# A last unit whose second block of positions is finished in two halves of 256 columns

## The chip, the cores and the metric

The kernel runs on one core of one Trainium2 chip. Its time is the device time in microseconds of one execution, and the median over several executions is quoted. The engines that matter here are TensorE (PE in the profile: matmuls; PEld is its weight load), VectorE (DVE), ScalarE (ACT), GpSimd (POOL) and SyncE (SP), whose queue issues every DMA of this kernel. Each engine takes its instructions in the order in which they stand in its own queue; between engines they wait on semaphores.

## The reference

One layer of a hybrid decoder block: a mixer (gated linear attention beside a short convolution) with a residual add, a SwiGLU feed-forward net with a residual add, and a last RMSNorm. 2048 positions, width 1024, feed-forward width 2816, float32. What the change touches is the end:

```python
        h2 = rmsnorm(x, norm2_g[l])
        ffn = (jax.nn.silu(h2 @ w_ffn_gate[l]) * (h2 @ w_ffn_up[l])) @ w_ffn_down[l]
        x = x + ffn
    return rmsnorm(x, norm_f_g)
```

with `rmsnorm(x, g) = x * rsqrt(mean(x * x) + 1e-6) * g`, the mean over the 1024 features of a position.

## The kernel before

**Layout.** Everything is held with features on the 128 partitions and positions along the free axis. `KD = 8` tiles of 128 features (index `d`) times `NB = 4` blocks of `PB = 512` positions make the whole residual stream. The feed-forward net is done for one half of the positions at a time (two blocks, `j = 0, 1`), so `y[d, j]` is a tile of 128 features by 512 positions; the tiles of one `d` lie side by side in one buffer (for `d = 7` in two).

**Products.** A float32 factor is split into a high and a low part, and a product of two 128-wide blocks is three matmuls (`product_step`, L366 to L368: high by high, high by low, low by high), each with a weight load of its own. Most matrix products go through `unit` (L370), a seven-product scheme in place of eight for a 2 by 2 block problem, with a few additions on GpSimd and VectorE. The down projection `ffn_down` (L921) takes the feed-forward width in four groups, and within a group four units, one for each pair of features `d0, d0 + 1`; what a unit gives is added to `y` (L965). In the last group of the last half the squares of each finished `y[d, j]` are summed into `ssq[j]` (L772 on ScalarE for the first, then L775 on ScalarE and L776 on GpSimd).

**The last unit.** `last_unit` (L995) is the last of these sixteen units. It does not use the seven-product scheme but eight plain products, so that the block `j = 0` is complete before `j = 1` is begun: four accumulations in PSUM (`j` outer, `r` inner, `d = 6 + r`), each of 2 by 3 calls of `product_step`, that is 18 matmuls of 512 columns. After each, VectorE adds the result to `y` (L1036), ScalarE squares it (L1038) and multiplies `y` by the norm's weight (`gain`, L1005; the gains of the tiles `d < 6` are done earlier, beside the unit ahead). The squares of `d = 6` are added to `ssq[j]` by GpSimd (L1041); those of `d = 7` come in by a second matmul. `norm` (L1007) adds over the partitions with a float32 matmul by a tile of ones into `tot` (L1010, L1011), takes the logarithm and the exponential on ScalarE (L184, L185), refines the result in one Newton step on VectorE (L186, L163, L164, L165) and leaves the factor in a PSUM tile `rb`, of which ScalarE makes a copy in SBUF (L1013) since GpSimd multiplies from SBUF. `scale` (L1016) multiplies the eight tiles of the block by the factor, two on GpSimd and six on VectorE, and each is stored as soon as it is done (L148).

**What sets the order.** The kernel is written as straight code for one core, and the tile layer's scheduler places the instructions of each engine by a timeline that it estimates while it builds the program; it may take an instruction ahead of others on its engine. `tc.issue_after(x)` holds the next instructions behind `x`. In the last unit before, only the accumulations of TensorE are chained in this way. ScalarE's table for logarithm and exponential is loaded (L1002) after the last weight split. The stores all go through SP's queue in one order, and ahead of each stands a wait for the store eight places earlier, whose semaphore it uses again.

Of the kernel before, what the change touches and what calls it, by code (L numbers as in the profile page):

```python
# [13 lines left out]
AF = mybir.ActivationFunctionType  # L14
ALU = mybir.AluOpType
# [3 lines left out]
P = 128  # L19
D = 1024  # L20
SEQ = 2048
PB = 512
NB = SEQ // PB
KD = D // P
# [7 lines left out]
EPS = 1e-6  # L32
# [14 lines left out]
C_G1, C_G2, C_GF, C_BG, C_GN, C_CW = 0, 8, 16, 24, 26, 27  # L47
# [4 lines left out]
def tile_hymba_block(ctx, tc, x, xt, win, wa, wgu, wout, wffn, wdown, wdown_first, small, out):  # L52
    nc = tc.nc
    act, dve, pool, pe = nc.scalar, nc.vector, nc.gpsimd, nc.tensor

    def pool_of(name, bufs, **kw):
# [19 lines left out]
    ones = const.tile([P, P], F32, name="ones")  # L76
# [4 lines left out]
        out=mask[:], in_=mask[:], compare_op=ALU.is_ge, fill=0.0, base=0,  # L81
# [65 lines left out]
    def store(dst, src):  # L147
        return nc.sync.dma_start(dst, src)  # L148
# [33 lines left out]
    def finish_rstd(v, tot, n, rb=None):  # L182
        l, y0 = bt("l"), bt("y0")
        act.activation(l[:], tot[:], AF.Ln, bias=eps[:], scale=1.0 / n)  # L184
# [173 lines left out]
        w["A22"] = weight_quarter(a22)  # L358
        return w

    def product_step(o, w, op, k, first):
        n = len(op)
        c = slice(k * P, (k + 1) * P)
        wh, wl = w[:, 0, c], w[:, 1, c]
        xh, xl = op[k][:, 0, :], op[k][:, 1, :]
        pe.matmul(o[:], wh, xh, start=first and k == 0, stop=False, skip_group_check=True)  # L366
        pe.matmul(o[:], wh, xl, start=False, stop=False, skip_group_check=True)  # L367
        return pe.matmul(o[:], wl, xh, start=False, stop=k == n - 1, skip_group_check=True)  # L368

    def unit(src, ops, into=None):  # L370

# [89 lines left out]
    rbs, raws, first_weights, last_load, rows, squares = {}, {}, {}, [], {}, {}  # L461
# [211 lines left out]
    done = set()  # L673
# [321 lines left out]
    def last_unit(src, ops, b12, y, ssq):  # L995


        raw = raw_weights(src)
        w = [weight_quarter(raw[:, i, :]) for i in (0, 1, 3, 2)]
        columns = (ops["B11"], ops["B21"]), (b12, ops["B22"])  # L1000
        with tc.issue_after(last_hi[0].ins):
            act.preload_act_table_set("natural_log_exp_and_others")  # L1002

        def gain(d, j):
            act.activation(y[d, j], y[d, j], AF.Copy, scale=col(C_GF + d))  # L1005

        def norm(j, q):  # L1007

            tot, rb = bank("tot"), bank("rb")
            pe.matmul(tot[:], ones[:], ssq[j][:], start=True, stop=False)  # L1010
            pe.matmul(tot[:], ones[:], q[:], start=False, stop=True)  # L1011
            finish_rstd(ssq[j], tot, D, rb)
            act.activation(ssq[j][:], rb[:], AF.Copy)  # L1013
            return rb

        def scale(j, rb):  # L1016
            for d in range(KD):
                eng, by = (pool, ssq[j]) if d in (2, 5) else (dve, rb)
                eng.tensor_tensor(y[d, j], y[d, j], by[:], ALU.mult)
                store(out[2 + j, :, d, :], y[d, j])  # L1020

        for d in range(KD - 2):
            for j in range(2):
                gain(d, j)
        q, rbs = {}, []
        for j in range(2):
            for r in range(2):
                o = bank()
                with ExitStack() as stack:
                    if j or r:  # L1030
                        stack.enter_context(tc.issue_after(done.ins))
                    for i in range(2):
                        for k in range(len(b12)):
                            done = product_step(o, w[2 * r + i], columns[j][i], k, i == 0)
                yy = y[KD - 2 + r, j]
                dve.tensor_tensor(yy, o[:], yy, ALU.add)  # L1036
                q[j] = tt("q")
                act.activation(q[j][:], yy, AF.Square)  # L1038
                gain(KD - 2 + r, j)
                if not r:  # L1040
                    pool.tensor_tensor(ssq[j][:], ssq[j][:], q[j][:], ALU.add)  # L1041
                if j and not r:
                    rbs.append(norm(0, q[0]))
        rbs.append(norm(1, q[1]))
        for j in range(2):
            scale(j, rbs[j])


    act.preload_act_table_set("natural_log_exp_and_others")
# [3 lines left out]
    ops, first, differences = build_h()  # L1053
# [132 lines left out]
```

## Time and profile before

| what | us |
|---|---|
| median of 3 executions | 2110.91 (2108.93 to 2113.38) |
| span of the profiled execution (first to last instruction) | 2109.1 |
| TensorE busy in it | 2033.1 (96%) |
| VectorE, ScalarE, GpSimd busy | 1418.4, 1014.1, 972.4 |
| last matmul of the last product starts | 2089.04 |
| first instruction of the last block's scalings | 2100.72 |
| last store is issued | 2105.30 |

Of the profiled execution the profile gives only the span; the median of the executions is 1.8 us above it. All times in the text below are microseconds from the start of that span. In the timeline a row has the start, the duration, the engine, the line and operation, what it writes and reads, how many instructions it stands for, and in brackets how long the engine was idle before it and what ended the wait. A matmul's duration includes its way through the array, so that one matmul begins before the one ahead has ended: the distance of the starts is what it costs.

### The profile page before, as it was taken

How to read it: one execution, taken by the hardware profiler on the slowest of the kernel's cores; microseconds unless marked ns; L12 is line 12 of the kernel's file. 1: busy time of each engine (PE TensorE's matmuls, PEld its weight loads, DVE VectorE, ACT ScalarE, POOL GpSimd, SP SyncE). 2: the span in 40 equal slices, each digit the busy share in tenths (PEclk: the TensorE clock that was granted, in tenths of full speed). 3: DMA queues.
4: the chain of work that ended last, by engine and by line, in shares of the span. 5: the costliest groups of instructions: out<-in, count | busy, mean ns of one | idle time of the engine just before them, and what ended most of it. 6: DMA issues, size and time to landing. Idle time of an engine off the chain costs nothing.

```text
span 2109.1 us, 26874 instructions
## 1 busy us (share of the span) xinstructions
PE 2033.1 (96%) x9133; PEld 1648.9 (78%) x9133; DVE 1418.4 (67%) x1983; ACT 1014.1 (48%) x1997; POOL 972.4 (46%) x703
## 2 busy tenths in 40 slices
PE   5999999999999999999999999999999989999996
PEld 4778888877888878788888878787888868877775
DVE  7669786549753786788786665554766666665564
ACT  5555455656542356445545443333554554543344
POOL 3436322222102464564464348764645544436774
PEclk9999999999999999999999999999999999999998
DMA  7349485425586872656545687697454535587763
GB/s 277 126 158 318 139 329 164 148 83 164 201 284 235 325 249 100 241 198 221 217 172 220 243 327 272 235 338 296 158 207 179 206 134 190 183 344 281 269 269 110
DMA packets 189241, 464.43 MB, mean 220 GB/s; under 512 B 19824, under 2 KB 65072, under 8 KB 179504
## 3 DMA queue, kind: packets, MB, share of 16 engines
q1 hardware_dynamic: 189104, 462.72, 60.4%
q8 instruction: 72, 1.18, 0.2%
q14 instruction: 65, 0.53, 0.1%
HBM read 297.49 MB, written 165.15 MB: 219 GB/s over the span
## 4 chain that ended last, share of the span: by engine, by line
PE 70%; DVE 8%; DMA 7%; ACT 3%; issue 3%; POOL 2%; SPq 0%; DVEq 0%; ACTq 0%; POOLq 0%
PE mm L366 21%; PE mm L368 21%; PE mm L367 21%; DVE wq L154 2%; DMA op<-shT 1%; DVE so L154 1%; PE mm L794 1%; DVE h L490 1%; PE mm L795 1%; PE mm L797 1%; DVE op L154 1%; DMA sx<-y 1%; ACT wq L153 1%; PE o_ps L718 1%; DMA shT<-so 1%
## 5 line engine op out<-in xcount | busy, mean ns | idle before, releaser
L366 PE MATMUL mm<-op,wq 128*128 128x512 f32 x2499 | 981.3, 395 | 23.8 <-DVE c L390 7.8
L368 PE MATMUL mm<-op,wq 128*128 128x512 f32 x2499 | 966.1, 392 | 12.6 <-DVE wq L154 11.9
L367 PE MATMUL mm<-op,wq 128*128 128x512 f32 x2499 | 976.0, 391 | 0.0
L154 DVE TENSOR_TENSOR wq<-raw,wq 128x512 fp32r<-128x512 f32 (+2 forms) x626 | 527.3, 849 | 329.9 <-ACT wq L153 324.3
L153 ACT ACTIVATE wq<-raw 128x512 fp32r<-128x512 f32 (+2 forms) x626 | 363.6, 587 | 555.8 <-PE mm L368 402.4
L366 PEld LDWEIGHTS mm<-op,wq 128*128 128x128 f32 x2499 | 470.8, 188 | 137.6 <-ACT wq L153 12.3
L368 PEld LDWEIGHTS mm<-op,wq 128*128 128x128 f32 x2499 | 470.5, 188 | 123.5 <-DVE wq L154 24.8
L367 PEld LDWEIGHTS mm<-op,wq 128*128 128x128 f32 x2499 | 471.2, 189 | 96.7 <-issue 1.0
L351 POOL TENSOR_TENSOR raw<-s,raw 128x512 f32<-128x512 f32 (+2 forms) x97 | 127.5, 1314 | 422.2 <-DVE wq L154 402.0
L390 DVE TENSOR_TENSOR c<-mm,c 128x512 f32<-128x512 f32 x267 | 183.0, 686 | 95.7 <-PE mm L368 93.0
L349 POOL TENSOR_TENSOR s<-raw 128x512 f32<-128x512 f32 (+2 forms) x97 | 130.2, 1343 | 216.2 <-DMA raw<-in_wffn_dram 88.8
L356 POOL TENSOR_TENSOR raw<-raw 128x512 f32<-128x512 f32 (+2 forms) x97 | 126.7, 1306 | 135.3 <-DVE wq L154 128.1
L386 ACT ACTIVATE c<-mm 128x512 f32<-128x512 f32 x267 | 154.7, 585 | 38.0 <-PE mm L368 36.8
L776 POOL TENSOR_TENSOR ssx<-ssx,q 128x512 f32<-128x512 f32 x52 | 76.5, 1483 | 156.0 <-ACT q L775 155.8
L350 POOL TENSOR_TENSOR raw<-raw 128x512 f32<-128x512 f32 (+2 forms) x97 | 135.1, 1393 | 4.1
L965 POOL TENSOR_TENSOR y<-c,y 128x512 f32<-128x512 f32 x66 | 98.7, 1499 | 49.0 <-DVE c L390 46.6
L154 DVE TENSOR_TENSOR so<-t,so 128x512 fp32r<-128x512 f32 x100 | 91.2, 918 | 25.9 <-ACT so L153 25.4
L153 ACT ACTIVATE wq<-s 128x512 fp32r<-128x512 f32 (+2 forms) x97 | 56.9, 586 | 93.5 <-PE mm L368 83.3
L794 PE MATMUL mm<-op,wq 128*128 128x512 f32 x256 | 100.9, 395 | 0.0
L795 PE MATMUL mm<-op,wq 128*128 128x512 f32 x256 | 99.8, 390 | 0.0
L154 DVE TENSOR_TENSOR wq<-s,wq 128x512 fp32r<-128x512 f32 (+2 forms) x97 | 84.1, 867 | 15.6 <-ACT wq L153 15.0
L153 ACT ACTIVATE so<-t 128x512 fp32r<-128x512 f32 x100 | 62.5, 627 | 41.8 <-DMA sa_T<-so 16.1
(177 smaller groups left out, 1885.0 us busy)
## 6 DMA issues: line engine op xcount, KB each, us to landing
raw<-in_wffn_dram SPq DMA_DIRECT2D x44, 1024.0 KB, 5.7
sa_T<-so SPq DMA_DIRECT2D x88, 512.0 KB, 5.3
op<-sa_T SPq DMA_DIRECT2D x88, 512.0 KB, 9.2
sa_B<-so SPq DMA_DIRECT2D x69, 512.0 KB, 3.4
op<-sa_B SPq DMA_DIRECT2D x69, 512.0 KB, 9.0
raw<-in_win_dram SPq DMA_DIRECT2D x23, 1024.0 KB, 5.5
raw<-in_wdown_dram SPq DMA_DIRECT2D x24, 768.0 KB, 6.2
sx<-y SPq DMA_DIRECT2D x48, 256.0 KB, 3.2
```

Source lines behind the costliest of these rows:

```text
L153: last_hi[:] = [act.activation(hi, src, AF.Copy)]
L154: return dve.tensor_tensor(lo, src, hi.bitcast(F32), ALU.subtract)
L349: pool.tensor_tensor(s1, a21, a22, ALU.add)
L350: pool.tensor_tensor(a21, a11, a21, ALU.subtract)
L351: pool.tensor_tensor(a11, s1, a11, ALU.subtract)
L356: pool.tensor_tensor(a12, a12, a11, ALU.subtract)
L366: pe.matmul(o[:], wh, xh, start=first and k == 0, stop=False, skip_group_check=True)
L367: pe.matmul(o[:], wh, xl, start=False, stop=False, skip_group_check=True)
L368: return pe.matmul(o[:], wl, xh, start=False, stop=k == n - 1, skip_group_check=True)
L386: act.activation(t[:], o[:], AF.Copy)
L390: dve.tensor_tensor(t[:], o[:], t[:], ALU.add)
L794: pe.matmul(o[e, j][:], wh, m[:, 0, :], start=k == 0, stop=False)
```

## The change

Four things are different, all in `last_unit`; the matmul helper `product_step` gets a slice of columns `s`.

1. The second block (`j = 1`) is worked in two halves of 256 columns, `sa` and `sb`. TensorE does both accumulations (`d = 6, 7`) of `sa`, then both of `sb`. Each half has its own `tot`, its own factor, its own scalings and its own stores. The first block stays whole.
2. Every instruction of this part on TensorE and on VectorE goes through `queued`, which holds it behind the one written before it on that engine. So their order is the order of the code: on TensorE also that of the matmuls that add up the squares (`summed`, L1037), which come in singly (the sum over the earlier tiles `ssq[j]`, then each of the two new squares), where before two came together.
3. The factor: the matmul's stationary tile holds 1/1024 in place of ones, the step that scaled `tot` and added epsilon (L186) is gone into the Newton step (L1048, L1051, L1057), which gives minus two times the factor; the norm's weight, times -1/2, is kept in a new tile `known`. GpSimd's additions of the squares of `d = 6` (L1041) are gone.
4. Scalings: of the first block GpSimd now does `d = 0` to `4` (before: 2 and 5), of each half of the second `d = 0` and `1`. Only those get the norm's weight from ScalarE beforehand (L1082); the others get it in the scaling itself, a VectorE instruction with two multiplications (L1069). There are 24 stores where there were 16: 8 of 256 KB and 16 of 128 KB.

TensorE, where the last unit begins. `mm_17758` is the accumulation of the unit ahead that is still open, `mm_17882` and `mm_17883` that of the last unit's first product (`d = 6`, first block), `mm_17906` that of its second (`d = 7`, first block), `ssx0` is `ssq[0]`. Before:

```order
L368 MATMUL mm_17882<-op_17474,wq_17860 128x512
L366 MATMUL mm_17906<-op_17452,wq_17863 128x512
L367 MATMUL mm_17906<-op_17452,wq_17863 128x512
L366 MATMUL mm_17758<-op_17488,wq_17755 128x512
...
L368 MATMUL mm_17758<-op_17492,wq_17755 128x512
L368 MATMUL mm_17906<-op_17452,wq_17863 128x512
L366 MATMUL mm_17906<-op_17454,wq_17863 128x512
```

and with the change:

```order
L368 MATMUL mm_17883<-op_17474,wq_17860 128x512
L366 MATMUL mm_17758<-op_17488,wq_17755 128x512
...
L368 MATMUL mm_17758<-op_17492,wq_17755 128x512
L1037 MATMUL tot_17880<-ssx0_17494,known_17870 128x512
L366 MATMUL mm_17906<-op_17452,wq_17863 128x512
L367 MATMUL mm_17906<-op_17452,wq_17863 128x512
```

The sum over `ssq[0]` now stands directly behind the last nine matmuls of the unit ahead and in front of the whole second product; before it stood behind three of the four products (`L1010`).

SP's queue, the stores at the end. `y_16095` and `y_16096` are the tiles `d = 0, 1`, `y_16203`, `y_16204`, `y_16301`, `y_16302` and `y_16395` are `d = 2` to `6`, `y_16396` and `y_16397` are `d = 7` of the first and the second block. Before, the sixteen stores are these eight of the first block and the like eight of the second:

```order
L148 DMA out_0_dram<-y_16095 128x512
L148 DMA out_0_dram<-y_16203 128x512
L148 DMA out_0_dram<-y_16096 128x512
L148 DMA out_0_dram<-y_16204 128x512
L148 DMA out_0_dram<-y_16301 128x512
L148 DMA out_0_dram<-y_16302 128x512
L148 DMA out_0_dram<-y_16395 128x512
L148 DMA out_0_dram<-y_16396 128x512
```

and with the change:

```order
L148 DMA out_0_dram<-y_16095 128x512
L148 DMA out_0_dram<-y_16302 128x512
L148 DMA out_0_dram<-y_16096 128x512
L148 DMA out_0_dram<-y_16203 128x512
L148 DMA out_0_dram<-y_16203 128x256
L148 DMA out_0_dram<-y_16204 128x512
L148 DMA out_0_dram<-y_16204 128x256
L148 DMA out_0_dram<-y_16301 128x512
...
L148 DMA out_0_dram<-y_16395 128x512
L148 DMA out_0_dram<-y_16396 128x512
...
L148 DMA out_0_dram<-y_16096 128x256
```

The eighth store is that of GpSimd's fifth scaling (`d = 4`, first block), and sixteen more stand behind it: the rest of `sa`, the tiles `d = 6, 7` of the first block, and all of `sb`.

VectorE, around the last residual add. `mm_17966` and `mm_18023` are the last products. Before:

```order
L165 SCALAR_TENSOR_TENSOR rb_17954<-l_17957,y0_17958 128x512
L1019 TENSOR_TENSOR y_16095<-y_16095,rb_17954 128x512
...
L1019 TENSOR_TENSOR y_16396<-y_16396,rb_17954 128x512
L1036 TENSOR_TENSOR y_16397<-mm_17966,y_16397 128x512
L186 TENSOR_SCALAR ssx1_17495<-tot_17989 128x512
```

and with the change:

```order
L1069 SCALAR_TENSOR_TENSOR y_16302<-y_16302,known_17870,rb_17980 128x512
L1048 TENSOR_TENSOR l_18018<-y0_18019 128x256
L1051 SCALAR_TENSOR_TENSOR l_18018<-tot_17881,l_18018 128x256
L1057 SCALAR_TENSOR_TENSOR rb_18045<-l_18018,y0_18019 128x256
L1031 TENSOR_TENSOR y_16397<-mm_18023,y_16397 128x256
L1069 SCALAR_TENSOR_TENSOR y_16203<-y_16203,known_17870,rb_18045 128x256
```

The last add (L1036, now L1031) stood behind the six scalings of the first block; now one scaling of that block and the factor of `sa` are ahead of it, and two scalings of the first block wait until after the last factor.

The diff, with the parts left out that only write the old order:

```diff
@@ -358,14 +358,14 @@
         w["A22"] = weight_quarter(a22)
         return w
 
-    def product_step(o, w, op, k, first):
+    def product_step(o, w, op, k, first, s=slice(0, PB)):
         n = len(op)
         c = slice(k * P, (k + 1) * P)
         wh, wl = w[:, 0, c], w[:, 1, c]
-        xh, xl = op[k][:, 0, :], op[k][:, 1, :]
-        pe.matmul(o[:], wh, xh, start=first and k == 0, stop=False, skip_group_check=True)
-        pe.matmul(o[:], wh, xl, start=False, stop=False, skip_group_check=True)
-        return pe.matmul(o[:], wl, xh, start=False, stop=k == n - 1, skip_group_check=True)
+        xh, xl = op[k][:, 0, s], op[k][:, 1, s]
+        pe.matmul(o[:, s], wh, xh, start=first and k == 0, stop=False, skip_group_check=True)
+        pe.matmul(o[:, s], wh, xl, start=False, stop=False, skip_group_check=True)
+        return pe.matmul(o[:, s], wl, xh, start=False, stop=k == n - 1, skip_group_check=True)
 
     def unit(src, ops, into=None):
 
@@ -1000,50 +1000,126 @@
         columns = (ops["B11"], ops["B21"]), (b12, ops["B22"])
         with tc.issue_after(last_hi[0].ins):
             act.preload_act_table_set("natural_log_exp_and_others")
-
...
+        known = bt("known", (P, P + KD))
+        means, gains = known[:, 0:P], known[:, P : P + KD]
+        dve.memset(means, 1.0 / D)
+        dve.tensor_scalar(gains, sml[:, C_GF : C_GF + KD], -0.5, None, ALU.mult)
+        halves = slice(0, PB // 2), slice(PB // 2, PB)
+        whole = slice(0, PB)
+        queues = {}
+
+        def queued(eng, issue):
+            with ExitStack() as stack:
+                if eng in queues:
+                    stack.enter_context(tc.issue_after(queues[eng].ins))
+                queues[eng] = issue()
+
+        def steps(o, r, j, s):
+            for i in range(2):
+                for k in range(len(b12)):
+                    queued(pe, lambda: product_step(o, w[2 * r + i], columns[j][i], k, i == 0, s))
+                    yield
+
+        def product(r, j, s):
+            o = bank()
+            for _ in steps(o, r, j, s):
+                pass
+            return o
+
+        def residual(o, r, j, s):
+            yy = y[KD - 2 + r, j][:, s]
+            queued(dve, lambda: dve.tensor_tensor(yy, o[:, s], yy, ALU.add))
+            q = tt("q")
+            act.activation(q[:, s], yy, AF.Square)
+            return q
+
+        def summed(tot, q, s, first=False, last=False):
+            queued(pe, lambda: pe.matmul(tot[:, s], means, q[:, s], start=first, stop=last))
+
+        def logs(j, tot, s):
+            l, y0 = bt("l"), bt("y0")
+            act.activation(l[:, s], tot[:, s], AF.Ln, bias=eps[:])
+            act.activation(y0[:, s], l[:, s], AF.Exp, scale=-0.5)
+            return l, y0
+
+        def factor(j, tot, s, l, y0):
+
+            rb = bank("rb")
+            queued(dve, lambda: dve.tensor_tensor(l[:, s], y0[:, s], y0[:, s], ALU.mult))
+            queued(
+                dve,
+                lambda: dve.scalar_tensor_tensor(
+                    l[:, s], tot[:, s], EPS, l[:, s], ALU.add, ALU.mult
+                ),
+            )
+            queued(
+                dve,
+                lambda: dve.scalar_tensor_tensor(
+                    rb[:, s], l[:, s], -3.0, y0[:, s], ALU.add, ALU.mult
+                ),
+            )
+            act.activation(ssq[j][:, s], rb[:, s], AF.Copy)
             return rb
 
+        def scale(ds, j, s, rb):
+            for d in ds:
+                yy, g = y[d, j][:, s], gains[:, d : d + 1]
+                queued(
+                    dve,
+                    lambda: dve.scalar_tensor_tensor(yy, yy, g, rb[:, s], ALU.mult, ALU.mult),
+                )
+                store(out[2 + j, :, d, s], yy)
+
+        def scale_beside(ds, j, s):
+            for d in ds:
+                yy = y[d, j][:, s]
+                pool.tensor_tensor(yy, yy, ssq[j][:, s], ALU.mult)
+                store(out[2 + j, :, d, s], yy)
+
+        beside = (0, 1, 2, 3, 4), (0, 1)
+        for j in range(2):
+            for d in beside[j]:
+                act.activation(y[d, j], y[d, j], AF.Copy, scale=gains[:, d : d + 1])
+
+        sa, sb = halves
+        tot = [bank("tot") for _ in range(3)]
+        o = product(0, 0, whole)
+        q6 = residual(o, 0, 0, whole)
+        summed(tot[0], ssq[0], whole, first=True)
+        o = product(1, 0, whole)
+        q7 = residual(o, 1, 0, whole)
+        o = product(0, 1, sa)
+        p6 = residual(o, 0, 1, sa)
+        summed(tot[0], q6, whole)
+        o = bank()
+        for n, _ in enumerate(steps(o, 1, 1, sa)):
+            if n == 2:
+                summed(tot[0], q7, whole, last=True)
+        l0 = logs(0, tot[0], whole)
+        p7 = residual(o, 1, 1, sa)
+        summed(tot[1], ssq[1], sa, first=True)
+        summed(tot[1], p6, sa)
+        rb0 = factor(0, tot[0], whole, *l0)
+        o = product(0, 1, sb)
+        scale_beside(beside[0], 0, whole)
+        r6 = residual(o, 0, 1, sb)
+        summed(tot[1], p7, sa, last=True)
+        l1 = logs(1, tot[1], sa)
+        summed(tot[2], ssq[1], sb, first=True)
+        o = product(1, 1, sb)
+        summed(tot[2], r6, sb)
+        scale((5,), 0, whole, rb0)
+        rb1 = factor(1, tot[1], sa, *l1)
+        r7 = residual(o, 1, 1, sb)
+        summed(tot[2], r7, sb, last=True)
+        l2 = logs(1, tot[2], sb)
+        scale((2, 3, 4, 5, 6), 1, sa, rb1)
+        scale_beside(beside[1], 1, sa)
+        rb2 = factor(1, tot[2], sb, *l2)
+        scale((6, 7), 0, whole, rb0)
+        scale((7,), 1, sa, rb1)
+        scale((2, 3, 4, 5, 6, 7), 1, sb, rb2)
+        scale_beside(beside[1], 1, sb)
 
 
     act.preload_act_table_set("natural_log_exp_and_others")
```

More of the change, by code (lines that the diff above doesn't have):

```diff
@@ L1002, in last_unit @@
             act.preload_act_table_set("natural_log_exp_and_others")
[L1004 to L1013, printed above, removed]
-            return rb
@@ L1016, in scale @@
[L1016 to L1025, printed above, removed]
-        for j in range(2):
[L1027 to L1043, printed above, removed]
@@ L1044, in last_unit @@
-        rbs.append(norm(1, q[1]))
-        for j in range(2):
-            scale(j, rbs[j])
+        known = bt("known", (P, P + KD))
[10 more added lines that the diff above has]
+                queues[eng] = issue()
```

## The prediction

> **What bounds the kernel now.** I read the page's engine totals and its chain of waits first, then the timeline of the last 36 us engine by engine, since the change touches nothing earlier that any engine waits for.
>
> ```profile
> span 2109.1 us, 26874 instructions
> PE 2033.1 (96%) x9133; PEld 1648.9 (78%) x9133; DVE 1418.4 (67%) x1983; ACT 1014.1 (48%) x1997; POOL 972.4 (46%) x703
> PE 70%; DVE 8%; DMA 7%; ACT 3%; issue 3%; POOL 2%; SPq 0%; DVEq 0%; ACTq 0%; POOLq 0%
> ```
>
> TensorE is the bound until its last product; what the change can win or lose lies in the end, here on TensorE, VectorE and SP's queue:
>
> ```profile
> 2083.43 1.02 PE L1010 MATMUL tot<-ssx,ones 128*128 128x512 f32 x2
> 2084.28 1.02 PE L1011 MATMUL tot<-q,ones 128*128 128x512 f32 x2
> 2089.04 0.39 PE L368 MATMUL mm<-op,wq 128*128 128x512 f32 x1
> 2094.82 1.67 PE L1011 MATMUL tot<-q,ones 128*128 128x512 f32 x2 [4.53 <-ACT q L1038]
> ...
> 2089.82 3.67 DVE L1019 TENSOR_TENSOR y<-y,rb 128x512 f32<-128x512 f32 x6 [0.66 <-ACT ssx L1013]
> 2093.41 0.69 DVE L1036 TENSOR_TENSOR y<-mm,y 128x512 f32<-128x512 f32 x1
> 2100.72 3.68 DVE L1019 TENSOR_TENSOR y<-y,rb 128x512 f32<-128x512 f32 x6 [0.66 <-ACT ssx L1013]
> ...
> 2090.54 0.34 SPq L148 DMA_DIRECT2D out_dram<-y  x1
> 2091.60 0.40 SPq L148 DMA_DIRECT2D out_dram<-y  x1
> 2093.09 0.54 SPq L148 DMA_DIRECT2D out_dram<-y  x1
> 2104.62 1.27 SPq L148 DMA_DIRECT2D out_dram<-y  x2
> 2105.30 0.59 SPq L148 DMA_DIRECT2D out_dram<-y  x1
> ...
> DMA to landing us min/median/max: 2.0/2.7/3.0
> ...
> 2104.00:2105.00 1.00, 0.00 (x0) 0.00 (x0) 0.40 (x1) 0.00 (x0) 0.00 (x0) 0.50 1.00 377
> ```
>
> The products are done at 2089.4, but the add of the last one starts at 2093.41, behind six scalings: 4.0 us. Then comes one serial chain of 7.3 us to 2100.72, then scalings and stores. The last store is issued at 2105.30, lands 3.0 later at 2108.3, and the span ends 0.8 after that. (The last row is a stretch of one microsecond: length, busy time by engine, the clock granted to TensorE, the DMA engines' busy share and GB/s; the engines that carry the stores are full there.)
>
> **What goes.** The 4.0 us behind the scalings, half the length of most links of the last chain, nine ScalarE gains, GpSimd's two additions (L1041) and two VectorE steps (L186). I give no gain to these by themselves: they count only if nothing later replaces them, and two things do.
>
> **First cost: TensorE waits for `ssq[0]`.** The sum over `ssq[0]` now stands directly behind the unit ahead (order of TensorE). `ssq[0]` is complete only when the last product of that very unit has been added, squared and summed. Before, that chain ran beside other products:
>
> ```profile
> 2073.45 0.39 PE L367 MATMUL mm<-op,wq 128*128 128x512 f32 x1
> 2073.68 0.39 PE L366 MATMUL mm<-op,wq 128*128 128x512 f32 x1
> 2075.49 0.39 PE L368 MATMUL mm<-op,wq 128*128 128x512 f32 x1
> ...
> 2075.92 0.53 ACT L153 ACTIVATE wq<-raw 128x384 fp32r<-128x384 f32 x1 [1.46 <-PE mm L368]
> 2076.46 1.28 ACT L1002 ACT_TABLE_LOAD   x1
> 2077.76 0.63 ACT L775 ACTIVATE q<-y 128x512 f32<-128x512 f32 x1
> ...
> 2078.47 1.30 POOL L776 TENSOR_TENSOR ssx<-ssx,q 128x512 f32<-128x512 f32 x1 [3.02 <-ACT q L775]
> ```
>
> ScalarE splits the last weights, loads its table and only then squares; GpSimd's add ends at 2079.77. With the change two matmuls no longer stand ahead of the unit's last nine (2073.68 less 0.45), so all of this comes 0.45 earlier: TensorE is done at 2075.49 + 0.39 - 0.45 = 2075.43, the add at 2079.32, and the sum starts at about 2079.37. TensorE idles 3.9 us, with the whole second product queued behind the wait, and everything else of the last unit behind that.
>
> **What that does to TensorE's clock.** The granted clock after other idle stretches, in windows cut where it changes (stretch, its length, then busy time by engine, clock):
>
> ```profile
> 60.91:64.33 3.42, 1.20 (x4) 0.67 (x4) 3.35 (x7) 3.42 (x8) 2.52 (x3) 1.00 0.58 218
> 64.33:67.74 3.41, 2.58 (x6) 2.10 (x7) 3.41 (x5) 3.41 (x10) 1.58 (x2) 0.50 0.28 48
> 67.74:71.16 3.42, 3.42 (x9) 2.65 (x9) 3.28 (x5) 3.39 (x10) 0.98 (x2) 0.50 0.97 383
> 1456.97:1460.38 3.41, 0.96 (x3) 0.49 (x3) 0.04 (x1) 1.18 (x3) 2.53 (x2) 1.00 0.01 5
> 1460.38:1463.79 3.41, 2.94 (x7) 2.36 (x8) 2.81 (x3) 1.96 (x4) 1.28 (x1) 0.50 0.47 125
> 1463.79:1467.20 3.41, 3.41 (x16) 2.80 (x16) 0.96 (x2) 1.74 (x4) 0.68 (x1) 1.00 0.92 340
> 2044.06:2047.47 3.41, 1.47 (x7) 0.89 (x5) 1.72 (x3) 2.55 (x5) 2.55 (x2) 1.00 0.00 0
> 2047.47:2050.90 3.43, 2.77 (x12) 2.31 (x13) 0.82 (x2) 2.10 (x5) 3.23 (x3) 1.00 0.63 224
> ```
>
> A window of 3.41 us in which TensorE was busy 1.20 or 0.96 us was followed by half clock, one with 1.47 was not. So somewhere between 1.94 and 2.21 idle microseconds in one window are enough; I take 2.05. A stretch of 3.95 us falls on a grid of 3.41 in any position; one window holds at least 2.05 of it in 2 x (3.41 - 2.05) + 3.95 - 3.41 = 3.26 of these 3.41, or 95 of 100. Half clock lasted one window where TensorE was busy 2.94 of it, and two where it was busy 2.58. For an idle stretch of 3.9 us that makes one window in six of ten positions (half of the busy part lost, 1.4 to 1.7 us) and two in the others (2.5 to 3.1). I take 1.6, with 0 and 3.1 as the ends.
>
> The Trainium skill (TensorE: Matmul & The Clock Gate, Part 1: The HAM clock gate) has the clock fall to half after at least one idle window of about 3.4 us on a free-running grid. Read strictly, 3.9 us hold a whole idle window in only (3.9 - 3.4) / 3.4 = 15 of 100 positions; by that the clock would mostly stay and the sum below end at +1.4, by the rows at +3.0. The trace disagrees with the page: windows still 28% and 35% busy sufficed.
>
> **TensorE up to the first factor.** One 512-column product is 2083.43 - 2079.35 = 4.08, a whole sum of squares 2084.28 - 2083.43 = 0.85, a half one 0.43 (estimate: half). A 256-column matmul isn't in the trace; the nearest row moves as long through the array and also has a weight load each:
>
> ```profile
> 2079.35 0.39 PE L366 MATMUL mm<-op,wq 128*128 128x512 f32 x1
> 293.32 1.05 PE L718 MATMUL o_ps<-vt,scores 128*128 128x128 f32 x8
> L718 PE MATMUL o_ps<-vt,scores 128*128 128x128 f32 x128 | 24.2, 275 | 0.0
> L366 PEld LDWEIGHTS mm<-op,wq 128*128 128x128 f32 x2499 | 470.8, 188 | 137.6 <-ACT wq L153 12.3 <-DVE c L390 8.6 <-ACT c L386 8.5
> 2085.64 0.67 ACT L184 ACTIVATE l<-tot,eps 128x512 f32<-128x512 f32 x1
> 2089.19 0.60 ACT L1013 ACTIVATE ssx<-rb 128x512 f32<-128x512 f32 x1 [2.22 <-DVE rb L165]
> 2089.87 2.50 POOL L1019 TENSOR_TENSOR y<-y,ssx 128x512 f32<-128x512 f32 x2 [3.51 <-ACT ssx L1013]
> L965 POOL TENSOR_TENSOR y<-c,y 128x512 f32<-128x512 f32 x66 | 98.7, 1499 | 49.0 <-DVE c L390 46.6
> ```
>
> (1.05 - 0.275) / 7 = 0.111 from start to start, so 2.0 for 18. The ends are 0.111 and 0.188, the time of one weight load if no two overlapped; I take 0.111, as those eight have loads of 0.19 too.
>
> So the last sum into the first block's `tot` ends at 2079.37 + 0.85 + 4.08 + 2.0 + 0.85 + 1.0 + 0.85 + 0.2 for the way out = 2089.2. From the logarithm to the end of the copy of the factor it is 2089.79 - 2085.64 = 4.15: the copy is there at 2093.35, where it was at 2089.79.
>
> **Second cost: the stores.** GpSimd's five scalings take 2.50 / 2 = 1.25 each (1.5 at the other end, L965): 2093.43 + 6.25 = 2099.7. The eighth store waits for the fifth, and sixteen stand behind it in SP's queue. Stores that are ready go out 0.50 apart (2091.60 to 2093.09, three steps). At the other end, 0.34 would be the bare issue (2090.54, the first of the burst) and 0.68 a queue held up by full DMA engines (2104.62 to 2105.30); these stores are half as large, so I take 0.50. The last is issued at 2099.7 + 16 x 0.50 = 2107.7, lands 2.0 later on an unfilled queue (2109.7), and the span ends at 2110.5. The semaphore that each store shares with the one eight places ahead is no wait: 8 x 0.50 = 4.0 is longer than a landing.
>
> Their data do not hold them up: TensorE's work from 2079.37 on is three whole sums, 4.08 for the second product, four half-width products and four half sums up to the last product's end, 2.6 + 4.1 + 8.0 + 1.7 = 16.4, so it ends at 2095.7; the last chain (add, square, sum, logarithm, exponential, three VectorE steps, at half the old durations or a little more) takes about 3.8, and nine scalings of 0.6 or 0.33 3.6: 2103.1, more than 3 us before SP gets to them. That slack is also what hides the wait for the last factor. The early setting of `known` costs nothing: it stands in a gap of VectorE 100 us earlier.
>
> **Sum.** 2110.5 against a span of 2109.1 is +1.4; with the clock's 1.6 it is +3.0, 2112.1. The median of the executions is 2110.91, 1.8 above that span, and I add the 3.0 to it: 2113.9. What a measurement of this kernel can tell from no change is about 0.2%, 4.2 us.
>
> **Rivals.**
> - *Two windows at half clock* (+1.2 on the forecast): +4.2, 2115.1. For it: the rows from 64.33 to 71.16. Chance 0.22, half of it above 0.2%.
> - *The clock stays*, because only a window idle throughout lowers it: +1.4, 2112.3. Against it: the rows above. It is what the Trainium skill's page (TensorE: Matmul & The Clock Gate) would give. Chance 0.08.
> - *Slower: the weight loads bind at 256 columns.* At 0.188 instead of 0.111 the 27 half-width matmuls ahead of the first factor cost 27 x 0.077 = 2.1 more, and all that follows shifts: +5.1, 2116.0. It passes 0.2% from about 0.155 per matmul on. For it: a load's own 188 ns; against: L718. Chance 0.10.
> - *The stores don't queue up*, because SP issues a 128 KB store in 0.34: then VectorE sets the end, 2103.1 plus two more stores, landing and the end, 3.8, and the clock's 1.6: 2108.5, so -0.6, 2110.3. For it: the bare issue; against: the 0.50 of ready stores. Chance 0.12.
>
> My forecast has the other 0.48. Cases beyond 0.2% are the third, half of the first and a tenth of the forecast's: 0.26 slower; faster by that needs two of my costs to be wrong at once: 0.04. The range goes from the last rival to the third, with a little of the spread of the three executions: 2110.0 to 2116.5.
>
> **What would show it.** TensorE idle for 3.9 us before the first L1037, ended by GpSimd's L776; the clock at 0.50 soon after; L367 of 256 columns about 0.11 apart; the factor's copy (L1061) near 2095; sixteen L148 rows about 0.50 apart to the end, with the last VectorE scaling some 3 us ahead of its store. I am wrong if TensorE doesn't wait there, if stores leave faster than 0.45 apart, or if the last store follows its scaling at once.

## The result, and the profile after

The changed kernel took 2116.79 us (median of 5 executions, 2114.97 to 2119.87) against 2110.8 for the kernel before beside it: a ratio of 1.0033, 95% interval 1.0021 to 1.0046. The profiled execution took 2116.79 with a span of 2115.0. A second comparison, on another chip, gave 1.0011 (1.0001 to 1.0021). So the change makes the kernel slower, by 0.33% in the one and 0.11% in the other.

The page of the changed kernel, the rows that answer to those of the kernel before:

```profile
span 2115.0 us, 26996 instructions
PE 2040.7 (96%) x9179; PEld 1656.4 (78%) x9179; DVE 1418.8 (67%) x1991; ACT 1009.2 (48%) x1993; POOL 973.6 (46%) x706
PE 78%; DVE 9%; DMA 6%; issue 2%; ACT 2%; POOL 1%; SPq 0%; DVEq 0%; ACTq 0%; POOLq 0%
```

The totals tell little. The timeline of the end does (start, duration, engine, line; in brackets the idle time ahead and what ended it):

```profile
2074.27 0.69 DVE L1031 TENSOR_TENSOR y<-mm,y 128x512 f32<-128x512 f32 x1 [2.51 <-PE mm L368]
2075.89 0.39 PE L368 MATMUL mm<-op,wq 128*128 128x512 f32 x1
2076.85 1.28 ACT L1002 ACT_TABLE_LOAD   x1
2078.14 0.63 ACT L775 ACTIVATE q<-y 128x512 f32<-128x512 f32 x1
2078.85 1.26 POOL L776 TENSOR_TENSOR ssx<-ssx,q 128x512 f32<-128x512 f32 x1 [2.54 <-ACT q L775]
2080.17 2.08 PE L1037 MATMUL tot<-ssx,known 128*128 128x512 f32 x2 [3.89 <-POOL ssx L776]
2087.63 0.28 PE L366 MATMUL mm<-op,wq 128*128 128x256 f32 x1
2089.66 0.28 PE L368 MATMUL mm<-op,wq 128*128 128x256 f32 x1
2096.41 0.60 ACT L1061 ACTIVATE ssx<-rb 128x512 f32<-128x512 f32 x1 [1.70 <-DVE rb L1057]
2097.09 6.59 POOL L1076 TENSOR_TENSOR y<-y,ssx 128x512 f32<-128x512 f32 x5 [16.97 <-ACT ssx L1061]
2098.39 1.52 DVE L1048 TENSOR_TENSOR l<-y 128x256 f32<-128x256 f32 x1 [0.47 <-ACT y L1042]
2100.41 0.92 DVE L1057 SCALAR_TENSOR_TENSOR rb<-l,y 128x256 f32<-128x256 f32 x1
2101.24 0.41 DVE L1031 TENSOR_TENSOR y<-mm,y 128x256 f32<-128x256 f32 x1
2102.16 1.18 PE L1037 MATMUL tot<-q,known 128*128 128x256 f32 x2 [1.91 <-ACT q L1033]
2106.16 4.14 DVE L1069 SCALAR_TENSOR_TENSOR y<-y,known,rb 128x512 f32<-128x512 f32 x9
2103.70 0.38 SPq L148 DMA_DIRECT2D out_dram<-y  x1
2106.15 0.40 SPq L148 DMA_DIRECT2D out_dram<-y  x1
2106.93 0.33 SPq L148 DMA_DIRECT2D out_dram<-y  x1
2107.59 0.33 SPq L148 DMA_DIRECT2D out_dram<-y  x1
2111.95 0.40 SPq L148 DMA_DIRECT2D out_dram<-y  x1
out_dram<-y SPq DMA_DIRECT2D x16, 128.0 KB, 1.8
```

TensorE waits 3.89 us for `ssq[0]`, ended by GpSimd's L776. The 18 matmuls of 256 columns from 2087.63 to 2089.66 are 2.03 / 17 = 0.119 apart. The first factor's copy starts at 2096.41. Sixteen store issues behind the eighth take 2111.95 - 2103.70 = 8.25. In two places among them SP stands idle, from 2106.55 to 2106.93 and from 2107.26 to 2107.59, until VectorE has scaled the tiles `d = 6` and `7` of the first block, which its order has behind the last factor (the first two of the nine scalings from 2106.16 on). VectorE ends its last scaling at 2110.30, so the last store still stands 1.65 behind it in SP's queue; it lands 1.8 later, and 1.3 after that the span ends. (The last row has the count, the size and the median time from issue to landing.)

The granted clock, in windows cut where it changes (stretch, length, busy time by engine, clock, DMA share, GB/s):

```profile
2074.93:2078.34 3.41, 1.34 (x6) 0.76 (x5) 1.19 (x3) 2.00 (x3) 1.31 (x2) 1.00 0.00 0
2078.34:2081.75 3.41, 1.58 (x3) 0.84 (x3) 0.00 (x0) 0.95 (x2) 1.26 (x1) 0.50 0.00 0
2081.75:2085.16 3.41, 3.41 (x9) 2.45 (x8) 0.00 (x0) 0.00 (x0) 0.00 (x0) 0.50 0.00 0
2085.16:2088.57 3.41, 3.41 (x20) 2.94 (x19) 0.69 (x1) 0.01 (x1) 0.00 (x0) 1.00 0.02 5
2098.82:2102.23 3.41, 1.50 (x12) 1.09 (x10) 3.22 (x6) 0.74 (x2) 3.41 (x3) 1.00 0.70 266
2102.23:2105.65 3.42, 1.11 (x2) 0.39 (x2) 2.88 (x7) 0.89 (x2) 2.81 (x4) 0.50 0.80 296
```

Half clock holds for two windows: the wait fell so that the first of them was itself more than half idle (busy 1.58), and a second one followed, busy throughout. Half clock comes back at 2102.23, behind TensorE's wait of 1.91 us for the last square, and the last sum (L1037 at 2102.16, two matmuls in the trace) takes 1.18 us; with the clock at 1.00 it takes 0.70 (the kernel with the wait filled, below, at 2102.84).

**A measure that the rest of the kernel does not disturb.** Executions of the same kernel differ by several microseconds, and in the profiles most of that lies ahead of the change: the first residual add of the last unit (L1036 before, L1031 after) comes at 2073.43, 2077.73 and 2077.71 in three profiles of the kernel before. I therefore compare, in the profiles, the time from that add to the end of the span, called the tail from here on. It is 2109.1 - 2073.43 = 35.7 before and 2115.0 - 2074.27 = 40.7 after: 5.0 more, of a forecast 3.0.

### The profile page after: what moved, and what is told of

Its sections match the earlier page's. It is cut to its first block, busy times and chain, and to the rows that moved or that the text cites. A ratio compares the mean times of both kernels' runs of the same rounds, so it can differ in the third digit from the quotient of the medians.

```text
span 2115.0 us, 26996 instructions
## 1 busy us (share of the span) xinstructions
PE 2040.7 (96%) x9179; PEld 1656.4 (78%) x9179; DVE 1418.8 (67%) x1991; ACT 1009.2 (48%) x1993; POOL 973.6 (46%) x706
## 3 DMA queue, kind: packets, MB, share of 16 engines
q8 instruction: 72, 1.18, 0.2%
## 4 chain that ended last, share of the span: by engine, by line
PE 78%; DVE 9%; DMA 6%; issue 2%; ACT 2%; POOL 1%; SPq 0%; DVEq 0%; ACTq 0%; POOLq 0%
PE mm L366 23%; PE mm L368 23%; PE mm L367 23%; DVE wq L154 2%; DVE h L490 2%; DVE op L154 1%; PE mm L794 1%; PE mm L795 1%; PE mm L797 1%; DVE so L154 1%; DMA raw<-in_wffn_dram 1%; DMA raw<-in_wdown_dram 1%; PE a_ps L558 1%; DMA h<-sfB 1%; DMA h<-in_xt_dram 1%
## 5 line engine op out<-in xcount | busy, mean ns | idle before, releaser
L776 POOL TENSOR_TENSOR ssx<-ssx,q 128x512 f32<-128x512 f32 x52 | 76.4, 1482 | 155.4 <-ACT q L775 155.2
```

## The experiments

| kernel | first residual add | span | from the one to the other | time, ratio to before (95%) |
|---|---|---|---|---|
| before, three profiles | 2073.43, 2077.73, 2077.71 | 2109.1, 2113.7, 2113.8 | 35.7, 36.0, 36.1 | |
| changed, two profiles | 2074.27, 2073.22 | 2115.0, 2113.9 | 40.7, 40.7 | 1.0033 (1.0021 to 1.0046), 1.0011 (1.0001 to 1.0021) |
| sum placed later | 2075.30 | 2109.1 | 33.8 | 0.9986 (0.9977 to 0.9994) |
| wait filled | 2076.18 | 2115.3 | 39.1 | 1.0013 (1.0004 to 1.0021) |
| two store queues | 2074.12 | 2114.2 | 40.1 | 1.0014 (1.0004 to 1.0023) |
| sum later and two queues | 2068.55 | 2101.7 | 33.2 | 0.9986 (0.9974 to 0.9997) |
| sum later, second block whole | 2077.65 | 2112.3 | 34.7 | 0.9986 (0.9977 to 0.9995) |
| sum later, GpSimd's old share | 2069.60 | 2103.8 | 34.2 | 0.9989 (0.9979 to 0.9999) |
| sum later, two queues, one SBUF input | 2072.09 | 2104.6 | 32.5 | 0.9983 (0.9973 to 0.9992) |

The ratios tell the kernels with the sum placed later from those without it. Among themselves these two groups overlap; finer differences are read from the fourth column (the tail) and the rows alone, with one profile for most kernels; tails of one and the same kernel differ by up to 0.4 in the first two lines.

My theory after the result: the wait for `ssq[0]` and the half clock behind it are the cost, and the store queue a second, smaller one. Rivals: the tail is held by stores and VectorE whatever TensorE does; or the two halves, or GpSimd's larger share, cost the time.

**The sum placed later.**

```diff
-        summed(tot[0], ssq[0], whole, first=True)
...
         p6 = residual(o, 0, 1, sa)
+        summed(tot[0], ssq[0], whole, first=True)
         summed(tot[0], q6, whole)
```

> One line moves: the product of ssq[0] into tot[0] is issued just ahead of that of q6, behind the half product (0, 1, sa), and no longer directly behind the unit ahead. Theory (the wait of TensorE for ssq[0] and the half clock that it sets off are the change's cost): the 3.89 us in which TensorE waits ahead of its first product with means are gone, the granted clock stays at 1.0 through the products, and the time from the first residual add to the end of the span falls from 40.7 us to 34.5 to 36 us, so 5 to 6 us below the changed kernel, a median of 2110.5 to 2112. Rival (the tail is held by the 32 store issues and VectorE's list, whatever TensorE does): the first factor's copy comes 5 us earlier, but the last store is issued less than 2 us earlier, and the median stays above 2114.5.

The tail is 33.8, even under the range of the theory, 6.9 less than in the changed kernel and 1.9 to 2.3 less than before. By the executions it is 0.14% faster than before. Of the 6.9, the wait is 3.9 and the half clock 2.4 (next experiment). The timeline and the clock windows of this kernel:

```profile
2076.65:2080.06 3.41, 3.41 (x16) 2.82 (x15) 1.16 (x2) 2.24 (x3) 0.67 (x1) 1.00 0.00 0
2080.34 1.29 POOL L776 TENSOR_TENSOR ssx<-ssx,q 128x512 f32<-128x512 f32 x1 [3.02 <-ACT q L775]
2083.37 1.02 PE L1037 MATMUL tot<-ssx,known 128*128 128x512 f32 x2
2090.85 0.60 ACT L1061 ACTIVATE ssx<-rb 128x512 f32<-128x512 f32 x1 [1.70 <-DVE rb L1057]
```

GpSimd's add is done at 2081.63, 1.7 us before TensorE comes to the sum: no wait is left, and the clock stays. The rival falls: stores and VectorE moved up with TensorE (there are 24 stores, not the 32 it speaks of). The place of this one sum, a pair of matmuls in the trace, turned a gain into a loss.

**The wait filled, for the clock alone.** The 18 matmuls are six calls of `product_step`; their sum is read by nobody.

```diff
+        idle = bank("idle")
+        for _ in range(6):
+            queued(pe, lambda: product_step(idle, w[0], columns[0][0], 0, True))
         summed(tot[0], ssq[0], whole, first=True)
```

> The changed kernel with 18 more products of 512 columns into a bank that nobody reads, issued ahead of the first product with means, so that TensorE works in most of the 3.89 us in which it waits. Nothing of the norm comes earlier by it; what it can change is the granted clock alone. Theory (half of the wait's cost is the half clock behind it): the clock stays at 1.0 behind the wait; the 18 products take 4.1 us at 0.227 each, 2.9 us of them inside the wait and up to 1.1 us ahead of the unit's last products; 2.5 us of half clock go and up to 1.2 us come, so the tail from the first residual add falls by 0.5 to 2.5 us from 40.7. Rival (the clock behind the wait is not on the path, since stores and VectorE end the kernel): the tail is the same or up to 1.2 us longer.

```profile
2079.70:2083.11 3.41, 2.56 (x12) 1.78 (x10) 0.81 (x2) 2.61 (x4) 1.21 (x1) 1.00 0.00 0
2083.11:2086.53 3.42, 3.31 (x13) 2.39 (x14) 0.00 (x0) 0.00 (x0) 0.06 (x1) 1.00 0.02 5
2083.22 1.13 PE L1037 MATMUL tot<-ssx,known 128*128 128x512 f32 x2 [0.96 <-POOL ssx L776]
2097.10 0.60 ACT L1061 ACTIVATE ssx<-rb 128x512 f32<-128x512 f32 x1 [1.70 <-DVE rb L1057]
```

The clock stays at 1.00. From the first sum to the factor's copy it takes 2097.10 - 2083.22 = 13.88; in the changed kernel 2096.41 - 2080.17 = 16.24. The half clock thus cost 2.36 us. In the other two profiles with the unfilled wait the same stretch takes 16.26 and 16.59 (2080.02 to 2096.28 with two store queues, 2079.12 to 2095.71 for the changed kernel again), so it cost 2.4 to 2.7. The sum itself starts 7.04 behind the first residual add instead of 5.90, because five of the fillers went ahead of the unit's last products (1.14). The tail gains 1.6, within the theory's range, and the rival's sign is wrong: the copy comes 1.2 earlier behind the first residual add, and the sixteen stores take 7.87 (2104.39 to 2112.26) without the two waits for VectorE, 0.4 less. The executions (1.0013 against 1.0033 and 1.0011) can't show a gain of this size, so it rests on the profiles.

**Two store queues.**

```diff
-                store(out[2 + j, :, d, s], yy)
+                by = act if s == sb else nc.sync
+                by.dma_start(out[2 + j, :, d, s], yy)
```

> The changed kernel with the six stores of the last half block's VectorE scalings issued by ScalarE and not by SyncE. Theory (SyncE's issues, 0.50 us apart, hold the end): VectorE ends its last scaling at about 2110.3, its store is issued 0.1 us behind it instead of 1.6 us, and the end comes 1 to 1.5 us earlier than the changed kernel. Rival (the transfers themselves or VectorE's list hold the end): less than 0.5 us.

```profile
2108.90 1.26 DVE L1069 SCALAR_TENSOR_TENSOR y<-y,known,rb 128x256 f32<-128x256 f32 x3
2108.24 3.20 ACTq L1072 DMA_DIRECT2D out_dram<-y  x6
2110.52 0.92 ACTq L1072 DMA_DIRECT2D out_dram<-y  x2
```

The tail is 40.1, 0.6 less than in the changed kernel: between the two. VectorE ends at 2110.16, and the last store is still issued 0.9 later: ScalarE's six issues take 0.5 each as SP's do, while VectorE makes a tile every 0.39. A second queue shortens the line, but only by what VectorE leaves.

**Both together.** The edits of the first and the third.

> The first and the third of these edits together: the product of ssq[0] behind the half product, and the last six stores of VectorE from ScalarE. Theory (the wait and the store queue are two costs one behind the other): both gains add up, 6 to 7.5 us below the changed kernel, a median of 2109 to 2110.8, level with the kernel before or up to 2 us below it. Rival (once TensorE does not wait, VectorE's list of scalings with a norm in two halves ends late by itself and the queue no longer matters): the same as the first edit alone within 0.5 us.

The tail is 33.2: the queue is again worth 0.6 on top of the 6.9 of the sum placed later. The two gains add up, as the theory said, and the median of 2110.22 lies in its range; the rival's half microsecond is just exceeded. Each 0.6 rests on one pair of profiles and is not far above the 0.4 by which tails of one kernel differ. The executions alone could not tell this kernel from the one with the sum placed later (both 0.9986).

**The changed kernel again.** Unedited.

> The changed kernel once more, unedited, beside the three edits of this group on the same chip. The time from the first residual add to the end of the span is 40.7 us again, within 0.5, with TensorE waiting 3.9 us for ssq[0]. The earlier profile of it lost 1.3 us more than the kernel before by a half clock behind the wait of 2.6 us at 2045 us, far ahead of the change: if that is chance, this profile may be without it; if the change brings it, it is there again.

The tail is 40.7, the wait 3.90, half clock lasts two windows again. That the two tails agree to 0.1 is partly luck: the half clock costs 0.35 more than in the first profile, and the sixteen stores take 7.89 (2103.00 to 2110.89), 0.36 less, since none of them waits for VectorE. The half clock at 2047 us is there too, which led to the two profiles of the kernel before, below.

**The second block whole.** One `tot`, one factor and eight stores fewer; the order stays given, with three first-block scalings on VectorE ahead of the second factor.

```diff
-        o = product(0, 1, sa)
+        o = product(0, 1, whole)
...
-        scale((2, 3, 4, 5, 6, 7), 1, sb, rb2)
-        scale_beside(beside[1], 1, sb)
+        scale((2, 3, 4, 5, 6, 7), 1, whole, rb1)
+        scale_beside(beside[1], 1, whole)
```

> The kernel with the sum placed later, but with the second block in one piece of 512 columns and one norm for it: 24 fewer and wider instructions and 8 fewer stores, the order of TensorE and VectorE still given and GpSimd still with five scalings of the first block. From the rows of the runs so far: last product at 46.6 us behind TensorE's resumption, residual add 0.7, square 0.7, sum 0.5, logarithm and exponential 1.3, three steps of the factor 2.1, six scalings 4.0, store and end 3.1, so 59 against 60.4 with two halves. Theory (the two halves cost as much as they bring): within 1.5 us of the kernel with the sum placed later, on the faster side. Rival (the halves are what pays in that kernel): 2 us or more slower than it.

The tail is 34.7, 0.9 more than with two halves, within 1.5 as the theory said but on the other side; the executions show no difference. So, with one profile for each, the halves are worth about 1 us. The rows of this kernel show two things that my estimate lacked:

```profile
2093.91 0.69 DVE L1048 TENSOR_TENSOR l<-y 128x512 f32<-128x512 f32 x1 [5.36 <-ACT y L1042]
2095.36 0.70 DVE L1057 SCALAR_TENSOR_TENSOR rb<-l,y 128x512 f32<-128x512 f32 x1
2099.92 1.19 DVE L1048 TENSOR_TENSOR l<-y 128x512 f32<-128x512 f32 x1 [1.07 <-ACT y L1042]
2101.87 0.92 DVE L1057 SCALAR_TENSOR_TENSOR rb<-l,y 128x512 f32<-128x512 f32 x1
2106.57 2.51 SPq L148 DMA_DIRECT2D out_dram<-y  x4
2107.00:2109.00 2.00, 0.00 (x0) 0.00 (x0) 0.49 (x1) 0.00 (x0) 0.00 (x0) 0.50 1.02 383
```

L1048 and L1057 of the second norm take 1.19 and 0.92 beside GpSimd's scalings, those of the first 0.69 and 0.70 without; and the DMA engines are full at the end (the last row), and stores of 256 KB leave 0.55 to 0.69 apart.

**GpSimd's old share.**

```diff
-        beside = (0, 1, 2, 3, 4), (0, 1)
+        beside = (0, 1), (0, 1)
...
-        scale((6, 7), 0, whole, rb0)
+        scale((2, 3, 4, 6, 7), 0, whole, rb0)
```

> The kernel with the sum placed later, but GpSimd with two scalings of the first block, as in the kernel before, and VectorE with five more behind the second half's factor (three more than so far). Theory (VectorE's instructions with two inputs in SBUF wait while GpSimd works, 1.52 us for L1048 of 256 columns and 0.92 for L1057): with GpSimd idle there the L1048 of the second norm takes 0.43 us and L1057 0.44, 1.6 us earlier, against three more scalings of 0.67, so within 1 us of the kernel with the sum placed later. Rival (those durations have another cause and GpSimd's share is a plain gain): L1048 stays at 1.5 and the end is 2 us later.

```profile
2085.83 2.55 POOL L1076 TENSOR_TENSOR y<-y,ssx 128x512 f32<-128x512 f32 x2 [9.83 <-ACT ssx L1061]
2087.14 1.52 DVE L1048 TENSOR_TENSOR l<-y 128x256 f32<-128x256 f32 x1 [0.47 <-ACT y L1042]
2089.15 0.43 DVE L1057 SCALAR_TENSOR_TENSOR rb<-l,y 128x256 f32<-128x256 f32 x1
2092.10 0.43 DVE L1048 TENSOR_TENSOR l<-y 128x256 f32<-128x256 f32 x1
```

The end is only 0.4 later, for three more scalings on VectorE, as the theory said; of its rows one differs. L1048 of the second norm still takes 1.52, because GpSimd's second scaling runs until 2088.38 and it ends 0.28 behind that. L1057 falls on idle GpSimd and takes 0.43 instead of 0.92, and L1048 of the third norm 0.43. So these durations come from GpSimd, and its larger share is worth little, since VectorE pays for it in waiting.

**One SBUF input.** The square of `y0` goes to ScalarE, the middle product to PSUM; six stores from ScalarE as above.

```diff
-            queued(dve, lambda: dve.tensor_tensor(l[:, s], y0[:, s], y0[:, s], ALU.mult))
+            act.activation(l[:, s], y0[:, s], AF.Square)
...
-                    l[:, s], tot[:, s], EPS, l[:, s], ALU.add, ALU.mult
+                    rb[:, s], tot[:, s], EPS, l[:, s], ALU.add, ALU.mult
...
-                    rb[:, s], l[:, s], -3.0, y0[:, s], ALU.add, ALU.mult
+                    rb[:, s], rb[:, s], -3.0, y0[:, s], ALU.add, ALU.mult
```

> The kernel with the sum placed later and six stores from ScalarE, with two more edits in the factor: the square of y0 is taken by ScalarE and not by VectorE, and the middle product stands in PSUM, so that no VectorE instruction of a factor has two inputs in SBUF. Theory (contention with GpSimd holds VectorE's chain at the end): L1057 of 256 columns takes 0.43 us beside GpSimd and not 0.92, the chain behind the second norm starts 1.5 to 2 us earlier, and the time from the first residual add to the end falls from 33.2 us to 31.3 to 32.2, the fastest so far. Rival (the store issues hold the end by now): less than 0.5 us gained.

```profile
2088.25 6.23 POOL L1077 TENSOR_TENSOR y<-y,ssx 128x512 f32<-128x512 f32 x5 [9.83 <-ACT ssx L1061]
2090.55 0.43 DVE L1057 SCALAR_TENSOR_TENSOR rb<-rb,y 128x256 f32<-128x256 f32 x1
2094.96 4.14 DVE L1069 SCALAR_TENSOR_TENSOR y<-y,known,rb 128x512 f32<-128x512 f32 x9
2097.17 5.13 ACTq L1072 DMA_DIRECT2D out_dram<-y  x6
2097.00:2101.00 4.00, 0.00 (x0) 0.00 (x0) 2.10 (x6) 0.00 (x0) 0.21 (x1) 0.50 0.96 342
```

L1057 takes 0.43 with GpSimd at work, as the theory said, and VectorE is done 27.0 us behind the first residual add (2099.10 - 2072.09) instead of 28.7 (2097.29 - 2068.55) with the sum later and two queues: 1.7 earlier. This edit does not separate what L1048 gains by leaving VectorE from what L1057 gains by its operand. And the end comes only 0.6 earlier (32.5, outside the theory's 31.3 to 32.2): behind VectorE the DMA engines are 96% busy, ScalarE's six issues stretch to 5.1 us, and the last of them is issued 2.8 behind VectorE's end. So the theory's mechanism holds, and the rival names what limits its gain: by now the end belongs to the stores. The full DMA engines point at their transfers rather than their issue; no run tests that. This is the version to keep, by its tail: 0.17% faster than the kernel before (ratio 0.9983, 0.9973 to 0.9992) and faster than the changed one.

The Trainium skill (SBUF — State Buffer, Who interferes with whom) has VectorE and GpSimd share a port pair as an exclusive lock, which a VectorE instruction takes part in when two of its inputs lie in SBUF, and not with one. The traces agree: L1057 takes 0.92 with two and 0.43 with one, both beside GpSimd. By that rule the cost could have been foreseen from the operands of the factor's steps.

**The kernel before, twice more.**

> The kernel before, unedited, for a second profile. In its first profile the wait of 2.60 us at 2045.5 us left the granted clock at 1.00; in all nine profiles of the changed kernel and its variants the same wait is followed by 3.41 us at 0.50, which moves the first residual add from 25.3 to 26.4 to 26.7 us behind the wait. If that is the place of the wait in the clock's windows and so chance, some profile of the kernel before shows it too; if the change causes it, none does. From the first residual add to the end: 35.7 within 0.5 either way.

> As the run beside it: a third profile of the kernel before, for the same question.

The first of these two profiles, around the wait at 2048 us and at the end of the unit:

```profile
2048.13:2051.54 3.41, 0.83 (x5) 0.52 (x4) 2.46 (x4) 2.58 (x6) 2.92 (x3) 1.00 0.10 14
2051.54:2054.95 3.41, 3.41 (x10) 2.67 (x9) 0.07 (x1) 0.70 (x2) 2.43 (x3) 0.50 0.62 216
2077.73 0.69 DVE L1036 TENSOR_TENSOR y<-mm,y 128x512 f32<-128x512 f32 x1 [2.52 <-PE mm L368]
```

Both have the half clock that the first profile of it lacked. There the window of the wait was still busy 1.47, here 0.83. So the change does not cause it; the profile from which I forecast was one with this window missed. It is 1.5 us of luck in that profile (25.30 us from the end of the wait, at 2048.13, to the first residual add; 26.79 and 26.85 in these two), and the tails (36.0, 36.1) are as before.

## Why the prediction was right or wrong

Forecast were 2113.9 us, +3.0. Measured were 2116.79 at first and 2115.65 in the second comparison, +6.0 and +2.4 on the kernel before beside them, and +4.6 to +5.0 in the tail. The direction and the main mechanism were right: slower, through TensorE's wait for `ssq[0]`. The first measurement lies 0.3 us above the range. That the second lies near the forecast is luck, as its tail is as long as the first one's. The step that failed is the clock's term of the sum, which had one window at half clock where there were two; beside it failed the step that took the stores to be free of VectorE.

- **First cost, right.** 3.89 us for a forecast 3.9, ended by L776 as said; the later sum takes it away together with the clock's share and brings 6.9.
- **Clock, mechanism right, size wrong.** This is the term of the sum that failed most: 1.6 forecast, 2.36 measured (2.71 in the second profile). I took one window, at six in ten; all three profiles with the unfilled wait have two, 6.83 us. So the rival "two windows at half clock" (2115.1) came true. As far as these three show, the two cases are not a free draw either. The windows lie on one grid: half clock set off by the wait at 2045 to 2048 begins at 2047.62, and nine windows of 3.41 later comes the cut at 2078.34. TensorE's wait for `ssq[0]` starts 28.6 us behind the end of that one, and in the three profiles a cut fell 2.07, 2.08 and 2.83 us into it, where the rest of it spoils the following window. That the clock stays, by a rule that wants a window idle throughout, fell: a window 1.34 busy was enough. My own limit, between 1.94 and 2.21 idle microseconds, does not hold either: 1.91 (the window busy 1.50) were enough at 2102.23, while 1.94 were not in the profile that I read.
- **TensorE up to the first factor.** 0.119 instead of 0.111 per half-width matmul, 0.2 in all for 27. The filled kernel, without half clock, needs 13.88 + 0.60 from the first sum to the end of the copy, for a forecast 13.98: 0.5 off. Of the other 0.3 no single row accounts for it. The rival in which weight loads bind (0.188) fell.
- **GpSimd's five scalings:** 6.59 for 6.25. Two of them, beside VectorE's L1048 and L1057, took 1.45 each. With one SBUF input in those the five took 6.23: the forecast price was that of GpSimd undisturbed.
- **Stores.** 8.25 for 8.0, with two errors in it. Sixteen that are ready take 7.87 to 7.89, and the other 0.4 are SP's two waits for VectorE. So "their data do not hold them up", with more than 3 us to spare, was wrong. VectorE's end was forecast at 2103.1 and came at 2110.30, 7.2 later: the later start gives 0.8, the clock 2.4 and TensorE's other work up to its last product 1.0. The last residual add gives 1.4, as it waited behind L1057 of the second factor (TensorE then waited 1.91 us for it). The last chain gives 1.2 (5.0 for 3.8, with its sum at half clock and an L1048 of 0.99) and the nine scalings 0.4. I had priced L1048 and L1057 at half the width of instructions that run alone. So both chains ended within 2 us of each other: two queues brought 0.6, and VectorE 1.7 earlier, on top of them, another 0.6. "The stores don't queue up" fell.
- **The end.** 1.8 to land and 1.3 behind it, for 2.0 and 0.8: +0.25.

In sum, from the first residual add to the end: clock 0.76, the first factor 0.5, GpSimd 0.34, stores 0.25, the end 0.25, less than 0.1 left: the 2.0 by which the forecast was short of the first profile. The executions' two results, +0.33% and +0.11%, lie on both sides of the tail's +0.22% to +0.24%.

What remains open is why executions of one kernel range over more than 10 us (the kernel before 2106.7 to 2120.6 on the chips used); half-clock windows at other waits, which the profiles place differently from one to the next, are a likely part, but this was not tried.

## What to carry to other kernels

When an order is fixed by hand, a matmul whose operand comes through three other engines must stand behind enough work to cover that chain: here 4 us of wait, and 2.4 to 2.7 more for the clock, hung on the place of a single sum, and the other edits together were worth 2 us. Before more work goes to GpSimd, look for VectorE instructions beside it that read two tiles from SBUF, and move one operand to PSUM or the instruction to ScalarE. Where one profile is the reference, look which half-clock windows it happened to have.

## What was not expected of the hardware

- A VectorE multiplication of 256 columns with both inputs in SBUF took 0.43 us with GpSimd idle and up to 1.52 beside it: it ended 0.28 after a GpSimd instruction did.
- With the DMA engines full (0.96 and 1.02 in the rows above, at 342 and 383 GB/s), issues on either queue stretched from 0.4 to 0.6 and more, one of ScalarE's to 1.77. With one queue the changed kernel already had them 0.87 and 0.89 busy from 2104 to 2108 and from 2108 to 2112, which left a second queue little to win.
- The same wait of 2.6 us, at the same place of the program, was followed by half clock in eleven of twelve profiles and not in one. Counted over all windows of 3.41 us in the twelve profiles, full clock was followed by half behind each in which TensorE was busy up to 1.44 us, behind some with 1.47 to 1.9, and behind none above; half clock ended behind each with 2.84 us or more and behind none with 2.80 or less.
